# Decoder trunk: the key norm factors of eight heads as one set of rows

## The chip, the cores and the metric

One Trainium2 chip, one of its cores. The metric is the device time of one execution in microseconds (us), taken as the median of several runs. Engines: TensorE (PE, with its weight loads as PEld), VectorE (DVE), ScalarE (ACT), GpSimd (POOL) and SyncE (SP), whose queue issues nearly all DMAs.

## The reference

Two decoder layers over T = 528 tokens (16 learned meta tokens and 512 of the sequence), width 1024. Each layer normalises its input, projects it once, and runs two causal mixers side by side: a pooling mixer and a latent attention with 8 heads. The part that matters here is the norm of the keys in the attention:

```python
q = (c_q @ w_q_b).reshape(B, L, N_HEADS, QK_HEAD_DIM)          # QK_HEAD_DIM = 64 + 32
kv = (c_kv @ w_kv_b).reshape(B, L, N_HEADS, QK_NOPE_DIM + V_HEAD_DIM)
k_nope, v = kv[..., :QK_NOPE_DIM], kv[..., QK_NOPE_DIM:]
k_pe = jnp.broadcast_to(k_rope_raw[:, :, None, :], (B, L, N_HEADS, QK_ROPE_DIM))
k = jnp.concatenate([k_nope, k_pe], axis=-1)
q = rmsnorm(q, g_qn)
k = rmsnorm(k, g_kn)          # one factor for each token and head
...
x = x + W_out( sigmoid(g_pool) * y_pool + sigmoid(g_mla) * y_mla )
```

So each of 8 heads has 528 factors, 1/sqrt(mean(k*k) + eps), by which its keys are multiplied.

## The kernel before

All products run in float32 split into a high and a low part: each weight tile is a `whi`, `wlo` pair (L185, L186), each activation a pair too, and `mm3` (L190 to L192) issues three matrix products for each tile and column range. Activations lie with channels on the 128 partitions and tokens along the free side. Layer 0 works on 528 tokens in two halves of 264 columns, layer 1 (the last) on most projections with the 512 sequence tokens at once.

The order is written by hand in `Layer.go`: a generator (`stream`) yields the large products one after another with a cost each, and the attention's steps are put between them. `fill_now(ns)` runs so many nanoseconds of products before the next step, `after(ns, ...)` defers a step. The tile framework then schedules all engines' instructions with a timeline of its own, so small changes can move neighbours. Buffers rotate: `tmp` has 3, the PSUM tiles `mm` have 4, `S` (scores) 3, `raw` (weights as loaded) 3, `bc` 3.

The stage of the change is `qk_stats` (L653), once in each layer, after the queries' last product. The sums of squares of queries and keys are transposed to tokens on partitions (L672, L673), `newton` (L293 to L300) takes the inverse roots into `ny`, 128 partitions x 5 token groups x 16 (columns 0 to 7 the keys' heads, 8 to 15 the queries'). Group 4 holds the 16 meta tokens. The queries' factors stay like this (`nqs`). The keys' factors must become rows of 528 tokens, one for each head. For that, `qk_stats` makes two widened copies of the keys' factors, each a zero-filled tile (L692) with 5 groups of 97 columns, in which the four heads' factors stand in columns 0, 32, 64 and 96 (L694). `fill_now(9500)` follows. Then, for each of the two copies, `rows` transposes the five groups on TensorE (L404, L406 three times, L407) into two PSUM tiles, copies them with two activations (L409, L410) to a `tmp` tile of 97 partitions, and a DMA writes its rows 0, 32, 64 and 96 to DRAM (`kdr`, L700).

`spread_k(h)` (L707) reads one head's row from `kdr` back, broadcast to 128 partitions (`bc`, 264 KB): heads 0 and 1 at the end of the stage, each later one when `prep` of the head two before it runs. `prep(h)` (L711) multiplies the key parts by `bc` on VectorE (L718) and GpSimd (L719), splits the product into `kh` and `kl` (L280, L281, in `split`), splits the queries, and `head(h)` runs the scores (`S`, L190 to L192 through `mm3`) and the softmax. The products that run beside this stage are those of the pooling's up projection (`pu`, inputs `u`, `th`, `tl`, evacuated at L557) and of a gate (`zm`, inputs `hh`, `hl`, evacuated at L500 to L503).

SyncE's queue takes, in this stage, weight loads (`raw`, L114), the two writes of `kdr` and the broadcasts, in program order.

Of the kernel before, what the change touches and what calls it, by code (L numbers as in the profile page):

```python
# [9 lines left out]
F32 = mybir.dt.float32  # L10
# [8 lines left out]
P = 128  # L19
DEPTH = 2  # L20
# [3 lines left out]
T = SEQ + NM  # L24
# [3 lines left out]
H = 8  # L28
# [43 lines left out]
def trunk(ctx, tc, xT, pos, win, wkr, wqb, wkb, wvb, wgr, wpu, wmu, wout, gains, const, yT):  # L72
    nc = tc.nc
    pe, act, dve, gp, sp = nc.tensor, nc.scalar, nc.vector, nc.gpsimd, nc.sync
# [6 lines left out]
    dp = ctx.enter_context(tc.tile_pool(name="dp", bufs=1, space=bass.MemoryType.DRAM))  # L81
# [4 lines left out]
    def nm(s):  # L86
        uid[0] += 1
        return f"{s}_{uid[0]}"

    def slot(tag, dt=F32, bufs=1, w=W):  # L90
        return sl.tile([P, w], dt, tag=tag, name=nm(tag), bufs=bufs)

    def tmp(w=W):
        return tp.tile([P, w], F32, tag="tmp", name=nm("tmp"), bufs=3)
# [4 lines left out]
    def mmt():  # L99
        return pp.tile([P, 512], F32, tag="mm", name=nm("mm"), bufs=4)  # L100
# [173 lines left out]
    def fill_now(ns):  # L274
        end = clk[0] + ns
        while clk[0] < end and step():
            pass
# [15 lines left out]
    def newton(y, a, t):  # L293
        dve.tensor_single_scalar(y.bitcast(I32), a.bitcast(I32), 1, op=ALU.logical_shift_right)
        dve.tensor_scalar(y.bitcast(I32), y.bitcast(I32), -1.0, float(0x5F3759DF), op0=ALU.mult, op1=ALU.add)
        dve.tensor_scalar(a, a, -0.5, None, op0=ALU.mult)
        for _ in range(3):
            dve.tensor_mul(t, y, y)
            dve.tensor_mul(t, t, a)
            dve.scalar_tensor_tensor(out=y, in0=t, scalar=1.5, in1=y, op0=ALU.add, op1=ALU.mult)  # L300
# [13 lines left out]
        dve.tensor_scalar(tcos, tcos, -2.0, 1.0, op0=ALU.mult, op1=ALU.add)  # L314

    scr = dp.tile([P, 8, SEQ], F32, name="scr")
    kdr = [[dp.tile([4, T], F32, name=f"kdr{l}{s}") for s in range(2)] for l in range(DEPTH)]

    hbuf = [(slot(f"hh{k}", F32R), slot(f"hl{k}", F32R)) for k in range(8)]

    class Layer:
# [331 lines left out]
        def qk_stats(self):  # L653
            fill_now(LAG + 100)
            while self.sq:
                self.stat_go()
            st = self.st
            sts = tmp()
            assert self.nsq == [12, 12] and not self.sq
            if self.last:  # L660
                dve.memset(sts[0:16, 0:NM], 1.0)
                spans = [(8, 0, 0, NM), (16, 0, NM, HALF), (16, 1, HALF, T)]
            else:
                spans = [(16, 0, 0, HALF), (16, 1, HALF, T)]
            for r, s, a, b in spans:
                g, o_ = 32 * s, HALF * s
                act.activation(sts[0:r, a:b], st[s][g:g + r, a - o_:b - o_], AF.Copy)
                dve.tensor_add(sts[0:r, a:b], st[s][g + 64:g + 64 + r, a - o_:b - o_], sts[0:r, a:b])
            fill_now(2600)
            stp = mmt()  # L670
            for j in range(4):
                pe.transpose(stp[:, 16 * j:16 * j + 16], sts[0:16, NM + P * j:NM + P * (j + 1)], ident[0:16, 0:16])  # L672
            pe.transpose(stp[0:16, 64:80], sts[0:16, 0:NM], ident[0:16, 0:16])  # L673
            na = sm.tile([P, 5, 16], F32, tag="na", name=nm("na"))
            ny = sm.tile([P, 5, 16], F32, tag="ny", name=nm("ny"))
            nt = sm.tile([P, 5, 16], F32, tag="nt", name=nm("nt"))
            dve.memset(na[:, 4, :], 1.0)
            dve.scalar_tensor_tensor(out=na[:, 0:4, :], in0=stp[:, 0:64].rearrange("p (a b) -> p a b", a=4),
                                     scalar=1.0 / QK,
                                     in1=cst[:, C_ADD:C_ADD + 16].unsqueeze(1).to_broadcast([P, 4, 16]),  # L680
                                     op0=ALU.mult, op1=ALU.add)
            dve.scalar_tensor_tensor(out=na[0:16, 4, :], in0=stp[0:16, 64:80], scalar=1.0 / QK,
                                     in1=cst[0:16, C_ADD:C_ADD + 16], op0=ALU.mult, op1=ALU.add)
            dve.scalar_tensor_tensor(out=na[:, :, 8:16], in0=self.eps.unsqueeze(2).to_broadcast([P, 5, 8]), scalar=EPS,
                                     in1=na[:, :, 8:16], op0=ALU.mult, op1=ALU.add)
            newton(ny, na, nt)
            self.nqs = sm.tile([P, 5, 8], F32, tag="nqs", name=nm("nqs"))
            dve.tensor_scalar(self.nqs, ny[:, :, 8:16], -1.0 / math.sqrt(QK), None, op0=ALU.mult)
            ws = []
            for s in range(2):  # L690
                w = tmp()
                gp.memset(w, 0.0)  # L692
                v = w[:, 0:485].rearrange("p (j c) -> p j c", c=97)
                dve.tensor_copy(v[:, :, 0:97:32], ny[:, :, 4 * s:4 * s + 4])  # L694
                ws.append(v)
            fill_now(9500)
            for s, v in enumerate(ws):
                t = tmp()
                self.rows(v, 97, t[0:97, 0:T])
                sp.dma_start(kdr[self.l][s], t[0:97:32, 0:T])  # L700
            self.bcs = {}
            for h in range(2):
                self.spread_k(h)
            if not self.last:
                self.smeta = sm.tile([NM, 8, NM], F32, tag="smeta", name=nm("smeta"))

        def spread_k(self, h):  # L707
            self.bcs[h] = bc = slot("bc", bufs=3)
            sp.dma_start(bc, kdr[self.l][h // 4][h % 4:h % 4 + 1, :].partition_broadcast(P))

        def prep(self, h):  # L711
            p, odd = h // 2, h % 2
# [415 lines left out]
```

## Time and profile before

| | |
|---|---|
| median of 3 runs | 801.98 us (801.45 to 802.34) |
| the profiled execution | 802.28 us, span 800.5 us |
| granted TensorE clock | 1.000 |
| TensorE busy | 792.9 us, 99% of the span |
| VectorE, ScalarE, GpSimd busy | 527.4, 416.9, 196.4 us |
| HBM | 97 GB/s over the span |

The span runs from the first to the last instruction. A row of the chain of waits gives start, duration and what held the path (engine, tile, line of the kernel); a row of an engine's timeline gives start, busy time, engine, line, operation, the tile written and those read, and in brackets the idle time before it with what ended it. Matrix products overlap in the pipeline, so their busy times are longer than their distance from each other. In a row of one line's instructions the three numbers are the shortest, middle and longest duration in ns.

### The profile page before, as it was taken

Reading aid. Unit: us, or ns where it says so; the run is one execution under the profiler, and the core shown is the slowest. Engines: PE = TensorE matmul, PEld = TensorE weight load, DVE = VectorE, ACT = ScalarE, POOL = GpSimd, SP = SyncE. Lnnn points to the kernel's source line nnn. Section 1 sums busy time; section 2 is a strip of 40 time slices with the busy share of each in tenths; the row PEclk is TensorE's granted clock in tenths of the full one; section 3 lists DMA queues with packets and bytes.
Section 4 is the critical chain, followed back from the end, with each engine's and each line's share of the span. In section 5 each row is a group of like instructions: output and inputs, shape, how many; then the busy total and the mean of one; then the engine's idle time right before and its main releaser. Section 6 shows DMA issues by size and latency. Waiting matters only on the chain.

```text
span 800.5 us, 14638 instructions
## 1 busy us (share of the span) xinstructions
PE 792.9 (99%) x5339; PEld 714.0 (89%) x5339; DVE 527.4 (66%) x1140; ACT 416.9 (52%) x947; POOL 196.4 (25%) x266
## 2 busy tenths in 40 slices
PE   9999999999999999999999999999999999999998
PEld 8889999999999999999997997877788888887887
DVE  5568767437679887585354686665467889665942
ACT  7455645545556665543254456446455666654421
POOL 1024404103333322142000163022024333410600
PEclk9999999999999999999999999999999999999999
DMA  6223233424222222234642222334253322222372
GB/s 240 74 69 93 71 100 90 110 83 143 83 87 87 80 67 67 81 91 142 181 143 73 73 87 86 92 86 119 82 154 97 100 77 79 76 69 78 92 232 97
DMA packets 48872, 80.71 MB, mean 101 GB/s; under 512 B 5904, under 2 KB 14480, under 8 KB 48800
## 3 DMA queue, kind: packets, MB, share of 16 engines
q1 hardware_dynamic: 48656, 79.52, 33.5%
q8 instruction: 42, 0.69, 0.4%
q14 instruction: 30, 0.25, 0.1%
q10 hardware_dynamic: 144, 0.26, 0.1%
HBM read 73.40 MB, written 4.23 MB: 97 GB/s over the span
## 4 chain that ended last, share of the span: by engine, by line
PE 96%; DMA 2%; DVE 1%; ACT 1%; issue 0%; POOL 0%; POOLq 0%
PE mm L190 28%; PE mm L192 28%; PE mm L191 27%; PE mm L813 2%; PE S L191 2%; PE S L192 1%; PE S L190 1%; PE o L819 1%; PE o L818 1%; PE mm L363 1%; PE S L472 1%; DMA xb<-xT 1%; DMA bc<-kdr 1%; PE mm L430 0%; DMA rinv<-win 0%; PE mm L406 0%
## 5 line engine op out<-in xcount | busy, mean ns | idle before, releaser
L190 PE MATMUL mm<-hh,whi 128*128 128x264 f32 (+2 forms) x1096 | 346.0, 318 | 0.4 <-ACT racc L827 0.2
L191 PE MATMUL mm<-hl,whi 128*128 128x264 f32 (+2 forms) x1096 | 343.5, 314 | 0.0
L192 PE MATMUL mm<-hh,wlo 128*128 128x264 f32 (+2 forms) x1096 | 342.0, 315 | 0.0
L186 DVE TENSOR_TENSOR wlo<-raw,whi 128x512 fp32r<-128x512 f32 (+2 forms) x251 | 185.5, 743 | 118.1 <-ACT whi L185 110.8
L185 ACT ACTIVATE whi<-raw 128x512 fp32r<-128x512 f32 (+2 forms) x251 | 150.3, 602 | 186.2 <-PE mm L191 131.1
L190 PEld LDWEIGHTS mm<-hh,whi 128*128 128x128 f32 x1096 | 205.6, 188 | 13.8 <-ACT racc L827 0.5
L191 PEld LDWEIGHTS mm<-hl,whi 128*128 128x128 f32 x1096 | 206.2, 188 | 12.2 <-issue 0.4
L192 PEld LDWEIGHTS mm<-hh,wlo 128*128 128x128 f32 x1096 | 205.0, 188 | 12.7 <-issue 0.4
L719 POOL TENSOR_TENSOR tmp<-kp,bc 64x528 f32<-64x528 f32 x16 | 24.5, 1532 | 113.2 <-DMA bc<-kdr 77.9
L550 POOL TENSOR_TENSOR racc<-racc,tmp 128x264 f32<-128x264 f32 (+1 forms) x15 | 14.1, 942 | 143.1 <-ACT tmp L549 143.0
L791 POOL TENSOR_TENSOR pm<-pa,rs 128x16 f32<-128x16 f32 x32 | 11.6, 361 | 145.6 <-DVE rs L786 145.6
L901 POOL TENSOR_TENSOR tmp<-tmp,xb 128x264 f32<-128x264 f32 (+1 forms) x24 | 26.9, 1143 | 58.6 <-DVE tmp L899 33.0
L747 DVE CUSTOM_DVE_ANT_0 S<-S,maskw,nqs 128x272 f32<-128x272 f32 (+4 forms) x80 | 38.4, 498 | 1.6 <-PE S L192 1.2
L754 ACT ACTIVATE cq<-S,bia 128x400 f32<-128x400 f32 (+2 forms) x48 | 24.6, 516 | 21.5 <-DVE bia L781 11.9
L190 PE MATMUL mm<-u,whi 128*128 128x264 f32 (+1 forms) x108 | 35.3, 327 | 0.0
L192 PE MATMUL mm<-cq,wlo 128*128 128x264 f32 (+1 forms) x108 | 34.8, 323 | 0.0
L192 PE MATMUL mm<-u,wlo 128*128 128x264 f32 (+1 forms) x108 | 34.8, 322 | 0.0
L191 PE MATMUL mm<-cq,whi 128*128 128x264 f32 (+1 forms) x108 | 34.8, 322 | 0.0
L190 PE MATMUL mm<-cq,whi 128*128 128x264 f32 (+1 forms) x108 | 34.7, 322 | 0.0
L281 DVE TENSOR_TENSOR tl<-mm,th 128x512 fp32r<-128x512 f32 (+1 forms) x64 | 29.3, 482 | 6.8 <-ACT th L280 5.8
L793 POOL TENSOR_TENSOR cq<-cq,rs 128x384 f32<-128x384 f32 (+1 forms) x32 | 32.7, 1021 | 0.0
L280 ACT ACTIVATE th<-mm 128x512 fp32r<-128x512 f32 (+1 forms) x64 | 25.4, 433 | 10.7 <-PE mm L813 10.4
(262 smaller groups left out, 1383.6 us busy)
## 6 DMA issues: line engine op xcount, KB each, us to landing
raw<-win SPq DMA_DIRECT2D x143, 256.0 KB, 2.6
raw<-wout SPq DMA_DIRECT2D x32, 256.0 KB, 3.0
bc<-kdr SPq DMA_DIRECT2D x16, 264.0 KB, 3.7
raw<-wpu SPq DMA_DIRECT2D x16, 256.0 KB, 2.6
raw<-wmu SPq DMA_DIRECT2D x16, 256.0 KB, 2.7
raw<-wqb SPq DMA_DIRECT2D x12, 256.0 KB, 2.8
tmp<-xT SPq DMA_DIRECT2D x16, 132.0 KB, 3.0
tmp<-scr SPq DMA_DIRECT2D x7, 256.0 KB, 4.3
```

The costliest lines, as they stand in the source:

```text
L185: act.activation(hi[:, :n], raw[:, :n], AF.Copy)
L186: dve.tensor_sub(lo[:, :n], raw[:, :n], hi[:, :n].bitcast(F32))
L190: pe.matmul(out, wh, xh, start=start, stop=False)
L191: pe.matmul(out, wh, xl, start=False, stop=False)
L192: pe.matmul(out, wl, xh, start=False, stop=stop)
L280: act.activation(hi[:, a:b], src, AF.Copy)
L281: dve.tensor_sub(lo[:, a:b], src, hi[:, a:b].bitcast(F32))
L719: gp.tensor_mul(kf[r0:r0 + 64, :], self.kp[r0:r0 + 64, :], bc[r0:r0 + 64, :])
L747: dve.tensor_tensor_reduce(out=sv, in0=sv, in1=mask, scale=nqs[:, i, h:h + 1], scalar=3e38, op0=ALU.add, op1=ALU.min, accum_out=bia[:, c:c ...
L754: act.activation(pv, sv, AF.Exp, scale=-1.0, bias=bia[:, i:i + 1], accum_out=rs[:, c:c + 1])
L793: gp.tensor_mul(pt[i][:, NM:], pt[i][:, NM:], rs[:, i:i + 1].to_broadcast([P, n - NM]))
L901: gp.tensor_add(t[:, :b - a], t[:, :b - a], self.am[m][:, a:b])
```

## The change

The two widened copies, their zero fills and the second pass of `rows` go. The keys' factors, columns 0 to 7 of each group in `ny`, are transposed directly: one set of five transposes with 8 columns each, two activations on 8 partitions, and one DMA that writes all eight rows to one `kdr` tile of 8 x 528 for each layer. `spread_k` reads its row from there. `rows` itself is the same; it also serves `norm_sums`, with 34 columns, as before.

```diff
-    kdr = [[dp.tile([4, T], F32, name=f"kdr{l}{s}") for s in range(2)] for l in range(DEPTH)]
+    kdr = [dp.tile([H, T], F32, name=f"kdr{l}") for l in range(DEPTH)]
...
-            ws = []
-            for s in range(2):
-                w = tmp()
-                gp.memset(w, 0.0)
-                v = w[:, 0:485].rearrange("p (j c) -> p j c", c=97)
-                dve.tensor_copy(v[:, :, 0:97:32], ny[:, :, 4 * s:4 * s + 4])
-                ws.append(v)
             fill_now(9500)
-            for s, v in enumerate(ws):
-                t = tmp()
-                self.rows(v, 97, t[0:97, 0:T])
-                sp.dma_start(kdr[self.l][s], t[0:97:32, 0:T])
+            t = tmp()
+            self.rows(ny[:, :, 0:8], 8, t[0:8, 0:T])
+            sp.dma_start(kdr[self.l], t[0:8, 0:T])
             self.bcs = {}
             for h in range(2):
                 self.spread_k(h)
...
         def spread_k(self, h):
             self.bcs[h] = bc = slot("bc", bufs=3)
-            sp.dma_start(bc, kdr[self.l][h // 4][h % 4:h % 4 + 1, :].partition_broadcast(P))
+            sp.dma_start(bc, kdr[self.l][h:h + 1, :].partition_broadcast(P))
```

## The prediction

> **What bounds the kernel now.** The page comes first: its busy times, then the chain that ended last. The profiled execution took 802.28 us, 1.78 us of it outside its span of 800.5 us.
>
> ```profile
> span 800.5 us, 14638 instructions
> PE 792.9 (99%) x5339; PEld 714.0 (89%) x5339; DVE 527.4 (66%) x1140; ACT 416.9 (52%) x947; POOL 196.4 (25%) x266
> PE 96%; DMA 2%; DVE 1%; ACT 1%; issue 0%; POOL 0%; POOLq 0%
> ```
>
> TensorE works 99% of the span and carries 96% of the chain. So a time on TensorE counts one for one, and a time on VectorE, ScalarE or GpSimd counts only where TensorE waits for it. The two places to read are the factor stages, once per layer (near 175 us and 577 us): the statistics are transposed into rows, written to DRAM (`kdr`), read back as broadcasts (`bc`), multiplied into the keys and split (`kh`, `kl`), and then the first scores run. The chain of waits in the first layer, in order of time (start, duration, what):
>
> ```profile
> 174.47 0.18 PE mm L404
> 174.65 0.50 PE mm L406 x3
> ...
> 175.79 0.26 ACT whi L185
> 176.05 0.28 issue
> 176.33 0.26 ACT tmp L410
> 176.59 0.03 ACT xb L557
> 176.61 1.72 DMA kdr<-tmp
> 178.33 0.02 issue
> 178.35 4.70 DMA bc<-kdr
> ...
> 183.21 1.76 POOL tmp L719
> 184.97 0.02 issue
> 184.99 0.65 ACT kh L280
> 185.64 0.04 issue
> 185.69 0.58 PE S L190 x2
> 186.26 0.12 PE mm L192
> ```
>
> This chain leaves TensorE for ScalarE at 175.79 and comes back to it at 185.69: the first scores of layer 0 wait for the factor's round trip through DRAM. TensorE's own timeline gives the size of that wait:
>
> ```profile
> 185.69 0.58 PE L190 MATMUL S<-kh,qhl 128*128 128x272 f32 x2 [0.49 <-ACT kh L280]
> ```
>
> It idles 0.49 us there; the products that the order puts ahead of the scores hide the rest of the trip. In layer 1 the chain stays on TensorE through the same stage:
>
> ```profile
> 576.00 0.18 PE mm L404
> 576.18 0.50 PE mm L406 x3
> 576.68 0.11 PE mm L407
> ...
> 577.72 0.18 PE mm L404
> 577.91 0.50 PE mm L406 x3
> 578.41 0.11 PE mm L407
> ...
> 587.76 0.31 PE S L190 x2
> ```
>
> Both sets of five transposes stand on the path, and the scores at 587.76 wait for nothing. ScalarE's row for their operand shows the slack:
>
> ```profile
> 584.80 0.65 ACT L280 ACTIVATE kh<-tmp 128x528 fp32r<-128x528 f32 x1 [2.58 <-POOL tmp L719]
> ```
>
> `kh` is done at 585.45, 2.31 us ahead. So one edit meets two limits: layer 1 is bound by TensorE's work, layer 0 by a DMA chain.
>
> **The work that goes.** Off the path first: four zero fills on GpSimd and four copies on VectorE leave.
>
> ```profile
> L694 DVE COPY tmp<-ny x4: 171/172/174, 169.4 to 571.0; 128x20 f32<-128x20 f32 x4
> ```
>
> The copies are 4 x 0.17 us, the first of layer 0 begun at 169.4 us; the transposes that read them run at 174.47, because `fill_now(9500)` puts products ahead of them, not because the copies end late. The fills come ahead of the copies (same buffers) on an engine that is 25% busy. Cost and gain of both are zero; what hides them is those 5 us of products. Two of four activations per layer (L409, L410) also go, from a ScalarE that is 52% busy; the second pair never stood in the chain. Of `tmp` buffers a layer takes three fewer, and with three in rotation every later user gets the buffer it had.
>
> On TensorE ten transposes go, five per layer, and the ten left load 8 columns of weights instead of 97. No row shows 8 columns. The nearest is the same helper on 34 columns (the chain, earlier in layer 0):
>
> ```profile
> 40.41 0.12 PE mm L404
> 40.53 0.43 PE mm L406 x3
> 40.96 0.11 PE mm L407
> ```
>
> and the weight loads of L404 and of L472 (min, median, max in ns):
>
> ```profile
> L404 PEld LDWEIGHTS mm<-cst,tmp x6: 91/156/156, 40.3 to 577.7; 16*97 16x97 f32 x4, 16*34 16x34 f32 x2
> L472 PEld LDWEIGHTS S<-sq,cst x88: 92/96/98, 72.3 to 562.4; 128*16 128x16 f32 x88
> ```
>
> A set of 97 columns costs 0.18 + 0.50 + 0.11 = 0.79 us of the path, one of 34 columns 0.12 + 0.43 + 0.11 = 0.66. From 34 columns to 16 the load stays at 91 to 92 ns at best, so I take 0.66 for 8 columns; bounds are 0.79 (no cheaper) and 0.60 (the straight line through 97 and 34 carried on to 8). The Trainium skill (TensorE: Matmul & The Clock Gate, "Step-by-step: what each phase is for") says that the weight load's time scales with the column count. By that rule an 8-column load would be an estimated 91 x 8 / 34 = 21 ns, and five of them would take up to 0.35 us more off each set, an estimated gain of 0.7 us beyond my sum if the load alone set the pace. The 34- and 16-column rows speak against it: the load has a floor, and I leave that out.
>
> **Layer 1.** Two sets of 0.79 become one of 0.66: 1.58 - 0.66 = 0.92 us (bounds 0.79 and 0.98). The built program's order puts the first four transposes two products earlier and leaves the fifth, which the write waits for, where the first set's was. The gain counts in full if the scores still find `kh` ready. SyncE's queue there:
>
> ```profile
> 577.42 0.54 SPq L700 DMA_DIRECT2D kdr<-tmp  x1
> 579.14 0.33 SPq L709 DMA_DIRECT2D bc<-kdr  x1
> ```
>
> The second write stood between the first and the second broadcast; it goes, and three broadcasts follow each other at once, as they already do in layer 0. The first broadcast waits for the write (579.14 - 577.42 = 1.72 us), as before. TensorE comes 0.92 us earlier, so the slack falls from 2.31 to 1.39 us. The broadcasts' landing is between these ends:
>
> ```profile
> DMA to landing us min/median/max: 3.0/3.7/5.3
> ```
>
> In layer 1 the first one took about 3.1 us (issued 579.14, its reader on VectorE starts at 582.26):
>
> ```profile
> 582.26 0.70 DVE L718 TENSOR_TENSOR tmp<-kn,bc 64x528 f32<-64x528 f32 x1 [3.38 <-DMA bc<-kdr]
> ```
>
> At layer 0's 4.70 it would be 1.6 us later, just 0.2 us over the slack. I take no wait; the bound is that one is 0.2 us, or 0.8 us with a landing of 5.3.
>
> **Layer 0.** Here the saved TensorE time meets a wait. The order of the built program shows one move: the first scores now stand four 264-column products later (they follow the third weight pass of `hh3`, where they stood after the second product of `hh2`). A product is 0.12 us (row 186.26), four are 0.48. Without waits TensorE would come to the scores at 185.69 - 0.49 (the idle) - 0.92 (the work) + 0.48 (the four) = 184.76. The chain does not come that early. Up to the weight-split activation it gains what the first four transposes save: 0.18 + 0.50 - 0.12 - 0.43 = 0.13 us, since L185 is released by the product behind them and L410 by the fifth transpose. From there nothing is shortened: the write, the broadcast, GpSimd's multiply, the split. The second write left SyncE's queue, but the broadcast was waiting for the first one's landing (1.72 here, 1.72 in layer 1 where nothing stood between). So the scores start at 185.69 - 0.13 = 185.56 and TensorE idles 0.8 us instead of 0.49. What counts is the place in the work: at 185.56 four more products are done than before at 185.69. The gain is 0.13 + 0.48 = 0.61 us, not the 1.41 us (0.92 of work, 0.49 of idle) that the transposes promise. `kl` and the next scores keep their five products of distance.
>
> What is unknown is the write of eight rows on one tile. Rows for both sides: the four-row write, 1.72 us in both layers, and the 66 KB moves of 32 rows:
>
> ```profile
> qhl<-q SPq DMA_DIRECT2D x16, 66.0 KB, 2.0
> ```
>
> That bounds it by 1.72 and 2.0; eight rows of 16.5 KB lie by the first, and I take 1.72. The loss is at most 0.28 us, in layer 0 alone. The Trainium skill (DMA: Bandwidth & Descriptors, "Why a DMA increments its semaphore by 16 and not by 1") has it that a copy is spread over the largest number of engines up to 16 that divides its row counts: eight rows would use eight engines where four used four, one row each, and last no longer. No view here shows the engines of one write.
>
> **Sum.** 0.92 + 0.61 = 1.53 us. 802.28 - 1.53 = 800.75 for the profiled execution's kind; that run was 0.30 us over the median of 801.98, so against the median 801.98 - 1.53 = 800.45, said as 800.4. The difference that a measurement can tell is 0.2%, or 1.6 us: my forecast lies just inside that.
>
> **Rivals.**
> *The broadcast comes sooner (0.22).* In layer 0 the first broadcast took 4.70 us, in layer 1 3.1, the median is 3.7. Ahead of it stand a 256 KB weight load and, between the two, the second write, which goes. If that write was what held it by a microsecond, TensorE's wait vanishes and layer 0 gains 0.92 + 0.49 = 1.41. The whole is 2.33 us, 799.65. Against it: the weight load stays ahead, 8 KB are little.
> *The factors come later and take the gain back (0.08).* A write of 2.0 us and a broadcast of 5.3 in both layers: layer 0 loses 0.28 + 0.60, layer 1 is 0.28 + 2.2 later and beyond its slack by 1.1. The gain is 1.53 - 0.88 - 1.1, -0.4: 802.4, no difference to be told.
> *Slower (0.11).* The one larger write lands late, and both layers wait for it. Each microsecond costs layer 0 in full, layer 1 from 1.39 us on. The gain is gone at 1.5 us of lateness (a write of 3.2 us), and from 2.3 us on (4.0 us) it is slower by more than 1.6. At the 5.3 us of the slowest broadcast, 3.58 us late, it is 1.53 - 3.58 - 2.19: 4.2 us slower, 806.2. Against it: the 66 KB moves take 2.0.
> *The change does less on TensorE:* 0.79 for a set makes 0.79 in layer 1 and 0.48 in layer 0, 1.27 us and 800.7. This lies in the forecast's case.
>
> **The numbers.** The forecast has 0.59, split by the 1.6 us bound: its gain runs from 1.27 (sets no cheaper) to 1.75 (sets of 0.60, which make 0.98 and 0.67, and a broadcast 0.1 us sooner), 0.26 of it beyond 1.6 and 0.33 within. Faster: 0.26 + 0.22 = 0.48. Same: 0.33 + 0.08 = 0.41. Slower: 0.11. The range runs from 799.4 (the first rival with the cheapest sets, 0.06 in each layer, and 0.1 for the spread of the runs) to 801.7 (the forecast with the write and the broadcast late in layer 0, 0.88, and the runs' spread above their median, 802.34 - 801.98 = 0.36); left out are the slower rival and a part of the late one.
>
> **What would show it.** In the profile after: in each layer one L404, three L406 and one L407 with 8 rows out, a set of 0.66 us in the chain; four fewer GpSimd fills; in layer 0 the wait of the first scores for `kh` up to about 0.8 us, at 1 us earlier in TensorE's work; the broadcast about 1.7 us after the write; in layer 1 no wait at the first scores. The forecast is wrong if the wait in layer 0 is gone (sooner broadcast) or over 1.5 us (late write), or if a wait for `kh` appears in layer 1.

## The result and the profile after

| | before | after | ratio, 95% interval |
|---|---|---|---|
| first comparison, median | 801.71 us (8 runs) | 799.54 us (8 runs) | 0.9971 [0.9962, 0.9980] |
| second, another group of runs | 801.56 (20) | 800.20 (10) | 0.9974 [0.9965, 0.9984] |
| third | 801.33 (13) | 799.55 (9) | 0.9977 [0.9967, 0.9987] |

The change makes the kernel faster by 0.23 to 0.29% by the ratios, 1.4 to 2.2 us by the medians (the ratios are not formed from these medians and come to 1.8 to 2.3 us). The mean of all 27 runs after lies 1.9 us below that of all 41 before. Forecast were 1.53 us (0.19%), just inside what was taken for the smallest difference that can be told. The profiled execution took 799.36 us, its span is 797.6 us. Its page (span, busy times, chain by engine):

```profile
span 797.6 us, 14595 instructions
PE 790.3 (99%) x5329; PEld 711.8 (89%) x5329; DVE 528.1 (66%) x1136; ACT 416.0 (52%) x943; POOL 194.4 (24%) x262
PE 96%; DMA 2%; ACT 1%; DVE 1%; issue 0%; POOL 0%; ACTq 0%; POOLq 0%
```

Nothing else became the bound: TensorE still has 96% of the chain, with ten products fewer. The chain of waits through layer 0's stage (start, duration, what):

```profile
174.17 0.11 PE mm L404
174.28 0.42 PE mm L406 x3
...
175.35 0.63 ACT whi L185
175.98 0.16 ACT tmp L410
...
176.16 1.47 DMA kdr<-tmp
...
177.65 4.43 DMA bc<-kdr
...
182.21 1.79 POOL tmp L711
...
184.03 0.65 ACT kh L280
...
184.72 0.58 PE S L190 x2
```

It is the same chain as before, and TensorE waits at its end as before (its own timeline):

```profile
184.72 0.58 PE L190 MATMUL S<-kh,qhl 128*128 128x272 f32 x2 [0.41 <-ACT kh L280]
```

In layer 1 one set is left on the path, in two parts, and the first scores wait for nothing:

```profile
573.65 0.11 PE mm L404
573.76 0.42 PE mm L406 x3
...
574.65 0.11 PE mm L407
```

```profile
583.21 0.65 ACT L280 ACTIVATE kh<-tmp 128x528 fp32r<-128x528 f32 x1 [3.83 <-POOL tmp L711]
584.77 0.47 PE L190 MATMUL S<-kh,qhl 128*128 128x272 f32 x2
```

`kh` is ready at 583.86, the scores start at 584.77.

**Where the time sits.** Two marks in each layer enclose the stage: the first transpose of the statistics (L672) and the first group of transposed probabilities (L813 before, L805 after). Rows of the chain, before and then after:

```profile
162.63 0.16 PE mm L672
203.18 0.77 PE mm L813 x7
565.26 0.35 PE mm L672 x4
605.35 0.55 PE mm L813 x5
```

```profile
162.33 0.16 PE mm L672
201.74 0.76 PE mm L805 x7
563.38 0.35 PE mm L672 x4
602.51 0.55 PE mm L805 x5
```

The stage went from 40.55 to 39.41 us in layer 0 (1.14 us) and from 40.09 to 39.13 us in layer 1 (0.96 us). The first gain is almost twice what was forecast (0.61), the second is near the forecast 0.92. The other 0.8 us between the two spans are the start (0.30 us up to the first mark), the stretch between the stages (0.44) and what comes behind them (0.06).

**What the wait costs.** The number in brackets is the idle time from the end of one record to the start of the next. Here a matrix product's record lasts 0.28 us while the next one starts 0.12 us after it, so the bracket leaves out a part of the pause. TensorE's rows around layer 0's first scores, in the first trace of the kernel before and in a second one (e8 below):

```profile
184.92 0.28 PE L191 MATMUL mm<-hl,whi 128*128 128x264 f32 x1
185.69 0.58 PE L190 MATMUL S<-kh,qhl 128*128 128x272 f32 x2 [0.49 <-ACT kh L280]
186.10 0.28 PE L192 MATMUL mm<-hh,wlo 128*128 128x264 f32 x1
```

```profile
185.24 0.29 PE L191 MATMUL mm<-hl,whi 128*128 128x264 f32 x1
185.37 0.47 PE L190 MATMUL S<-kh,qhl 128*128 128x272 f32 x2
185.68 0.29 PE L192 MATMUL mm<-hh,wlo 128*128 128x264 f32 x1
```

In e8 nothing waits: `kh` is done 0.20 us ahead, the scores start 0.13 us after the product before them, and the next product 0.31 us after the scores. In the first trace these distances are 0.77 and 0.41 us, so the wait cost 0.64 + 0.10 = 0.74 us of TensorE's time, not the 0.49 of the bracket. In each of the other twelve traces the scores start 0.05 or 0.06 us after `kh` is done, so there TensorE waits for it, even where no bracket is shown. The marks and this cost were read in every run below:

| kernel | stage 0 | idle in brackets | cost of the wait | stage 0 without the cost | stage 1 |
|---|---|---|---|---|---|
| before, three traces | 40.55, 39.82, 39.96 | 0.49, 0, 0 | 0.74, 0, 0.16 | 39.81, 39.82, 39.80 | 40.09, 40.09, 40.09 |
| after, three traces | 39.41, 39.89, 39.43 | 0.41, 0.90, 0.43 | 0.66, 1.15, 0.69 | 38.75, 38.74, 38.74 | 39.13, 39.14, 39.13 |
| e1, adjacent rows | 40.93 | 0.87 | 1.12 | 39.81 | 40.12 |
| e2, two writes | 39.06 | 0 | 0.31 | 38.75 | 39.14 |
| e3, two narrow sets | 40.79 | 0.90 | 1.16 | 39.63 | 39.76 |
| e4, one wide set | 40.09 | 0.93 | 1.19 | 38.90 | 39.28 |
| e5, rows two apart | 39.41 | 0.37 | 0.63 | 38.78 | 39.16 |
| e6 and e11, fill_now(10200) | 38.33, 38.57 | 0, 0.25 | 0.26, 0.50 | 38.07, 38.07 | 39.14, 39.14 |

(us.) Without the cost of the wait each kernel's stage 0 repeats to 0.02 us; with the brackets alone taken off, the kernel before would have 40.06, 39.82 and 39.96. The stage of e6 and e11 holds 313 products, that of the kernel after 319, so these two are not to be compared: six products have moved behind its second mark. Two other stretches of TensorE's work repeat to 0.02 us in all thirteen traces: start of the norm sums to the first mark 137.98 to 138.00, second mark of layer 1 to the last head's end 117.18 or 117.19. The stretch between the two stages does not: 361.56 to 362.08.

### The profile page after: what moved, and what is told of

It reads as the page before. It is cut to its first block, busy times and chain, and to the rows that moved or that the text cites. A ratio compares the mean times of both kernels' runs of the same rounds, so it can differ in the third digit from the quotient of the medians.

```text
span 797.6 us, 14595 instructions
## 1 busy us (share of the span) xinstructions
PE 790.3 (99%) x5329; PEld 711.8 (89%) x5329; DVE 528.1 (66%) x1136; ACT 416.0 (52%) x943; POOL 194.4 (24%) x262
## 4 chain that ended last, share of the span: by engine, by line
PE 96%; DMA 2%; ACT 1%; DVE 1%; issue 0%; POOL 0%; ACTq 0%; POOLq 0%
PE mm L190 28%; PE mm L192 27%; PE mm L191 27%; PE mm L805 2%; PE S L191 2%; PE S L192 2%; PE S L190 1%; PE o L811 1%; PE o L810 1%; PE mm L363 1%; PE S L472 1%; DMA xb<-xT 1%; DMA bc<-kdr 1%; PE mm L430 0%; DMA rinv<-win 0%; DMA raw<-wmu 0%
```

## The experiments

Theories. A: the write of the kernel before was slow to issue because its source rows lie apart; that it does not do so any more made layer 0's chain shorter than forecast. Rivals: B, eight rows on one DMA go faster than four; C, the second write in the queue held the first broadcast; D, the gain comes from narrow weights, not from the count of sets. Then E and F, on the broadcast's landing.

**e1, adjacent rows.** The kernel before, with

```diff
-                dve.tensor_copy(v[:, :, 0:97:32], ny[:, :, 4 * s:4 * s + 4])
+                dve.tensor_copy(v[:, :, 0:4], ny[:, :, 4 * s:4 * s + 4])
...
-                sp.dma_start(kdr[self.l][s], t[0:97:32, 0:T])
+                sp.dma_start(kdr[self.l][s], t[0:4, 0:T])
```

> The kernel before, with the four heads' factors in columns 0 to 3 of each widened copy instead of 0, 32, 64 and 96, and the two writes from rows 0 to 3. Still 97 columns, two sets, two writes. The order puts layer 0's first scores two 264-column products earlier than before. Theory A (the write of the kernel before was slow to issue because its source rows lie 32 partitions apart): the write's issue takes 0.3 us instead of 0.54 to 0.59, and in layer 0 the broadcast is issued 1.5 us after the write instead of 1.74; the two products fewer leave the wait for the key operand at about 0.5 us, so the time is that of the kernel before within 0.2 us. Theory B (eight rows go faster than four): issue 0.54, 1.74 us, the wait 0.73 us, 0.25 us slower than before.

Measured: 802.34 us, ratio 1.0012 [1.0003, 1.0021], slower by 0.7 us by the medians. The write's issue on SyncE's queue, in ns, for the kernel before, e1, the kernel after, e4 and e5 (rows 32 apart, adjacent, adjacent, 12 apart, 2 apart):

```profile
L700 SPq DMA_DIRECT2D kdr<-tmp x4: 537/542/595, 176.6 to 579.5; - x4
```

```profile
L700 SPq DMA_DIRECT2D kdr<-tmp x4: 267/320/330, 176.4 to 579.5; - x4
```

```profile
L692 SPq DMA_DIRECT2D kdr<-tmp x2: 292/321/350, 176.2 to 575.1; - x2
```

```profile
L696 SPq DMA_DIRECT2D kdr<-tmp x2: 677/696/714, 176.3 to 576.3; - x2
```

```profile
L696 SPq DMA_DIRECT2D kdr<-tmp x2: 670/688/707, 175.9 to 575.3; - x2
```

In e1 the broadcast was issued 1.42 us after the write (176.36 to 177.78) instead of 1.74. So A holds for the write: adjacent rows alone bring it, with four rows and two writes, and B falls. The idle time of 0.87 us was missed (0.5 expected), and the likely cause is in two rows, GpSimd's multiply in e1 and in the kernel after:

```profile
182.38 2.46 POOL L719 TENSOR_TENSOR tmp<-kp,bc 64x528 f32<-64x528 f32 x1 [40.10 <-PE mm L191]
```

```profile
182.21 1.78 POOL L711 TENSOR_TENSOR tmp<-kp,bc 64x528 f32<-64x528 f32 x1 [40.93 <-DMA bc<-kdr]
```

VectorE's timeline in e1 in that time:

```profile
182.34 0.70 DVE L718 TENSOR_TENSOR tmp<-kn,bc 64x528 f32<-64x528 f32 x1 [5.45 <-DMA bc<-kdr]
182.97 0.68 DVE L186 TENSOR_TENSOR wlo<-raw,whi 128x512 fp32r<-128x512 f32 x1
```

A weight's low part follows VectorE's multiply at once, and GpSimd's multiply takes 0.68 us longer, just the length of that operation. In the kernel after no second VectorE operation stands there. The Trainium skill (SBUF — State Buffer, "Who interferes with whom") has it that a VectorE instruction with two SBUF inputs contends with a GpSimd instruction that reads SBUF, and that this contention is an exclusive lock. These rows agree: one operation of 0.68 us for 0.68 us.

**e2, two writes.** The kernel after, with

```diff
-            sp.dma_start(kdr[self.l], t[0:8, 0:T])
+            for s in range(2):
+                sp.dma_start(kdr[self.l][s], t[4 * s:4 * s + 4, 0:T])
```

and two `kdr` tiles read as before.

> The kernel after, but the eight rows are written by two DMAs of four adjacent rows, to two DRAM tiles as before. One narrow set of transposes. The order puts layer 0's first scores eight products (0.97 us) later than in the kernel after. Theory A: issue 0.3 us for each write, broadcast 1.5 us after the first; the eight products cover the rest of the DMA chain, no wait for the key operand in layer 0, 0.4 us faster than the kernel after, 2.2 to 2.6 us faster than before. Theory C (the second write in the queue is what held the broadcast of the kernel before): the first broadcast lands 0.3 us or more later than in the kernel after (4.7 us after its issue, not 4.43); the time is the same as in theory A since 0.5 us of cover are left.

Measured: 799.15 us, ratio 0.9975 [0.9966, 0.9984], 2.5 us faster by the medians. No idle time in brackets, but the scores start 0.34 us after the product before them, so a wait of 0.31 us is left, where none was expected. Stage 0 is 39.06, and without the wait 38.75, the same as the kernel after. The broadcast came 1.42 us after the first write (176.94 to 178.36) and landed 4.51 us later in the chain, between 4.43 and 4.92 of the kernel after. One trace in such a spread could not show the 0.3 us that C expects. But the kernel before, with its second write, has the two shortest landings of all traces with a load between write and broadcast (e8 and e9), so C falls. Layer 1's stage is the same as in the kernel after (39.14): one DMA instead of two is no part of the gain on TensorE.

**e3, two narrow sets.** The kernel after, with

```diff
-            t = tmp()
-            self.rows(ny[:, :, 0:8], 8, t[0:8, 0:T])
-            sp.dma_start(kdr[self.l], t[0:8, 0:T])
+            for s in range(2):
+                t = tmp()
+                self.rows(ny[:, :, 4 * s:4 * s + 4], 4, t[0:4, 0:T])
+                sp.dma_start(kdr[self.l][s], t[0:4, 0:T])
```

> The kernel after, but two narrow sets of five transposes with 4 columns each, two pairs of activations and two writes of four adjacent rows: no widened copies, but nothing merged. The order puts layer 0's first scores six products (0.73 us) earlier than in the kernel after. Theory A: layer 1 gives back one set, 0.64 us, and keeps 0.3 of its gain of 0.95; in layer 0 the chain is as short as in the kernel after and the wait grows to 0.5 us, which with six products fewer keeps 0.4 of its 1.14 us. Sum 0.7 us faster than before. Theory D (the gain is the narrow weights, not the count of sets): 2 us faster than before, layer 1 keeps 0.7 us or more.

Measured: 801.22 us, ratio 1.0000 [0.9991, 1.0009], 0.4 us faster by the medians, where A expected 0.7. Layer 1 keeps 0.33 of 0.96 us, as A said (0.3), not 0.7 (D). The 0.4 us of layer 0 did not come: the idle time was 0.90 us, with GpSimd's multiply beside two VectorE operations again (2.35 us in its row of the chain), and its products alone took 0.26 us more than 38.74 + 0.63, which was not taken apart.

**e4, one wide set.** The kernel after, with one widened copy of 85 columns:

```diff
+            w = tmp()
+            gp.memset(w, 0.0)
+            v = w[:, 0:425].rearrange("p (j c) -> p j c", c=85)
+            dve.tensor_copy(v[:, :, 0:85:12], ny[:, :, 0:8])
             fill_now(9500)
             t = tmp()
-            self.rows(ny[:, :, 0:8], 8, t[0:8, 0:T])
-            sp.dma_start(kdr[self.l], t[0:8, 0:T])
+            self.rows(v, 85, t[0:85, 0:T])
+            sp.dma_start(kdr[self.l], t[0:85:12, 0:T])
```

> The kernel after, but the eight heads' factors stand in columns 0, 12, ... 84 of one widened copy of 85 columns, so that there is one set of wide transposes and one write whose eight source rows lie 12 partitions apart. The order puts layer 0's first scores one product later than in the kernel after. Theory A: the write's issue takes 0.5 us or more and the broadcast comes 1.74 us or more after it; a set costs 0.76 us; layer 0 gains 0.9, layer 1 0.83, 1.7 us faster than before. Theory B (eight rows go faster than four): issue 0.3 us, 1.5 us, layer 0 gains 1.1, 1.95 us faster. Theory D: 0.3 us faster than before.

Measured: 800.01 us, ratio 0.9983 [0.9974, 0.9992], 1.64 us faster by the medians. Layer 1 gains 0.81 (0.83 expected); D is out. The issue takes 0.68 to 0.71 us, the broadcast came 1.81 us after the write (176.28 to 178.09): with eight rows apart the write is slower than with four. Layer 0 gained 0.46 instead of 0.9, with an idle time of 0.93 us and a broadcast of 4.78.

From e3 and e4 the parts of layer 1's 0.96 us: a second narrow set 0.63 us (39.76 - 39.13), the width 0.33 us in two sets (40.09 - 39.76) or 0.15 in one of 85 columns.

**e5, rows two apart.** The same with 15 columns, `v[:, :, 0:15:2]`, and `t[0:15:2, 0:T]` as the source.

> The kernel after, but the eight heads' factors stand in columns 0, 2, ... 14 of one widened copy of 15 columns: narrow weights, one set, one write, its source rows two partitions apart. The order puts layer 0's first scores one product later than in the kernel after, layer 1's one later too. Theory A1 (any step between the source rows makes the write slow to issue, and what follows it slow): issue 0.7 us, broadcast issued 1.8 us after the write and landing 4.7 to 4.8 us later as with a step of 12; the wait for the key operand about 0.9 us, layer 0 gains 0.5 us over before, layer 1 0.95, 1.4 us faster than before. Theory A2 (only rows far apart are slow): issue 0.3, 1.5 and 4.45 us as in the kernel after, wait 0.3 us, layer 0 gains 1.2, 2.2 us faster than before.

Measured: 800.18 us, ratio 0.9984 [0.9974, 0.9993], 1.4 us faster by the medians. The issue is as slow as with a step of 12 (row above), and the broadcast came 1.87 us after the write (175.93 to 177.80): a step of 2 costs as much as one of 12, so it is not the distance that counts (A1). But in this trace the broadcast landed in 4.15 us, not 4.7 to 4.8, and stage 0 was as short as in the first trace of the kernel after. So the broadcast's landing does not follow from the write, and is a question by itself.

**e6, another place of the transposes.** The kernel after with `fill_now(10200)` for 9500.

> The kernel after with fill_now(10200) in place of 9500. In layer 0 the transposes move six products later, eighty products instead of 78 stand between them and the first scores, and on SyncE's queue no weight load stands between the write and the broadcasts; layer 1's order is as in the kernel after. Theory E (the first broadcast of layer 0 takes 4.43 us because a 256 KB load is ahead of it): it lands in 3.1 to 3.5 us, the first scores wait for nothing, layer 0 gains 0.4 us more, 2.5 us faster than before. Rival (a load ahead of the write only moves the delay from the broadcast to the write): broadcast 2.3 us after the write, 3.3 us to land, a wait of about 0.3 us, 2.2 us faster than before.

Measured: 799.08 us, ratio 0.9963 [0.9950, 0.9976], the fastest so far. SyncE's queue and the first scores:

```profile
177.56 0.37 SPq L692 DMA_DIRECT2D kdr<-tmp  x1
179.89 1.29 SPq L701 DMA_DIRECT2D bc<-kdr  x3
```

```profile
183.06 0.70 DVE L710 TENSOR_TENSOR tmp<-kn,bc 64x528 f32<-64x528 f32 x1 [2.34 <-DMA bc<-kdr]
```

```profile
185.58 0.65 ACT L280 ACTIVATE kh<-tmp 128x528 fp32r<-128x528 f32 x1 [2.39 <-POOL tmp L711]
```

```profile
185.99 0.28 PE L191 MATMUL mm<-hl,whi 128*128 128x264 f32 x1
186.28 0.57 PE L190 MATMUL S<-kh,qhl 128*128 128x272 f32 x2
```

Without a load between write and broadcast, the broadcast's first reader starts 3.17 us after its issue; but the write, now with a load issued 0.38 us ahead of it (177.18), takes 2.33 us. Both E and its rival fit: the load would delay whichever DMA stands behind it. This is argued from these rows, not shown. In layer 1, where a load is issued 1.63 us ahead of the write both here and in the kernel after, the write took 1.47 us here and 2.27 there, so the order in the queue does not settle its time. Write and broadcast together take 5.50 us, 5.94 in the kernel after's first trace. The idle time in brackets is gone, but the wait is not, against E: `kh` is done at 186.23, the scores start 0.05 us later and 0.29 us after the product before them. The wait still costs 0.26 us, near the rival's 0.3.

**e7, the kernel after again**, unchanged.

> The kernel after, unchanged, for a second trace. The stage of layer 0 and that of layer 1 take what they took (the gains of 1.14 and 0.95 us over before); the start of the run and the stretch behind the first layer's stage, which were 0.3 and 0.46 us shorter than before, show by how much they vary: if the change shortened them they come out the same, if it is spread they differ by a few tenths.

Measured: 800.20 us, ratio 0.9974 [0.9965, 0.9984]. Layer 1's stage came out the same (39.14). Layer 0's did not: 39.89, with an idle time of 0.90 us. The chain names it:

```profile
176.46 1.48 DMA kdr<-tmp
177.93 0.02 issue
177.95 4.92 DMA bc<-kdr
```

The write took what it took in the first trace (1.47), the broadcast half a microsecond more. The start (24.65 us against 24.35) and the stretch between the stages (361.89 against 361.64) were both longer than in the first trace, so what they had gained there is at least in part spread.

**e8 and e9, the kernel before again**, unchanged.

> The kernel before, unchanged, for a second trace of it. Theory F (the first broadcast of layer 0 lands at varying times from run to run, 4.2 to 4.9 us after its issue, in either kernel; the change has no part in it; what the change shortens is the write, by a quarter of a microsecond): the write leads the broadcast by 1.72 to 1.74 us in both layers as in the first trace, the landing differs from 4.70 by some tenths and layer 0's stage, from the statistics' first transpose to the first transposed probabilities, by as much from 40.55 us; layer 1's stage is 40.09 us again. Rival (the change also shortens the broadcast): 4.70 and 40.55 again.

> The same, for a third trace: theory F again a landing of its own between 4.2 and 4.9 us; the rival 4.70 and 40.55.

Measured: 801.52 and 802.12 us. SyncE's queue in e8 and the broadcast's first reader (the first scores are shown further up):

```profile
176.94 0.60 SPq L700 DMA_DIRECT2D kdr<-tmp  x1
177.64 0.34 SPq L114 DMA_DIRECT2D raw<-win  x1
...
178.68 1.32 SPq L709 DMA_DIRECT2D bc<-kdr  x3
```

```profile
182.60 0.70 DVE L718 TENSOR_TENSOR tmp<-kn,bc 64x528 f32<-64x528 f32 x1 [1.16 <-DMA bc<-kdr]
```

The write leads the broadcast by 1.74 us in layer 0 in all three traces of before. The broadcast's first reader starts 4.72, 3.92 and 4.14 us after its issue, and the wait costs 0.74, 0 and 0.16 us. F holds in that the landing varies in both kernels (after: 4.45, 4.94, 4.46), but more widely than its 4.2 to 4.9 us. From the write's issue to that reader it is 6.46, 5.66 and 5.88 us before, 5.94, 6.43 and 5.96 us after: on the mean 6.0 and 6.1, the same. So on these means the write's quarter of a microsecond does not reach the keys, though three traces each that scatter by half a microsecond and more could hide it. Theory A explains the write, not the stage. That the broadcast, issued sooner, only waits longer behind the same weight load is the likely reading; it is argued from e6, not shown by itself.

**e10, the kernel after a third time, and e11, fill_now(10200) again**, on one chip.

> The kernel after, unchanged, for a third trace, and timed on the same chip as the next. Theory F: write to broadcast 1.47 to 1.49 us in layer 0 as in both traces so far, landing between 4.2 and 4.9, layer 0's stage between 39.1 and 39.9 us, layer 1's 39.14. About 2 us faster than before. Rival: landing near 4.43.

> The kernel after with fill_now(10200), again, beside the kernel after on one chip. Theory F with the wait gone: layer 0's stage is 38.3 us again whatever the broadcast's landing, since nothing waits for it, and the time is 0.7 to 1.3 us less than that of the kernel after. Rival (the first trace was a lucky landing): a wait for the key operand of some tenths, the time of the kernel after.

Measured: e10 799.55 us (799.08 to 800.65), ratio 0.9977 [0.9967, 0.9987]; e11 798.69 us (798.50 to 799.65), ratio 0.9962 [0.9950, 0.9975]. e10: write to broadcast 1.50 us, stage 0 39.43. e11 is 0.86 us below e10 by the medians, as e6 was 1.1 us below e7, also on one chip. The landing was not without effect, against F's word: TensorE sat idle 0.25 us, and the wait cost 0.50. So `fill_now(10200)` is the version that is faster than both kernels in the two places where they ran side by side; against the kernel before the intervals of the two overlap. Of its gain over the kernel after, the shorter wait is 0.45 us on the means (0.38 against 0.83 us); the rest was not taken apart.

## Why the prediction was right or wrong

**Layer 1: right.** 0.92 forecast, 0.95 to 0.96 measured in three traces each. A set of 8 columns takes 0.11 + 0.42 + 0.11 = 0.64 us of the path against 0.66 taken from 34 columns. No wait came; the slack by TensorE's own row fell to 0.91 us in the first trace (by the same row, 587.60, it was 2.15 before, so 1.23 was to be left), since the write there took 2.27 us (issued 575.09, broadcast 577.36; 1.88 and 1.90 in e7 and e10), a delay for which the prediction had no term. Its cause is open: with the same order in layer 1, e6 and e11 show 1.47 and 1.48 us. The first trace's rows:

```profile
575.09 0.29 SPq L692 DMA_DIRECT2D kdr<-tmp  x1
577.36 1.27 SPq L701 DMA_DIRECT2D bc<-kdr  x3
```

**The weights' floor: right.** The prediction let the load's time stay near 91 ns instead of falling with the columns. By the Trainium skill (TensorE: Matmul & The Clock Gate, "Step-by-step: what each phase is for") 8 columns were an estimated 21 ns. The loads of L404 and L406 in the kernel after, 34 columns and 8:

```profile
L404 PEld LDWEIGHTS mm<-cst,tmp x2: 91/92/92, 40.0 to 444.8; 16*34 16x34 f32 x2
L404 PEld LDWEIGHTS mm<-cst,ny x2: 77/78/78, 174.1 to 573.6; 16*8 16x8 f32 x2
L406 PEld LDWEIGHTS mm<-cst,ny x6: 83/87/87, 174.2 to 573.8; 128*8 128x8 f32 x6
```

The time falls with the columns, but only by 14 ns from 34 to 8, so the trace does not bear out the 21 ns.

**Layer 0: the mechanism right, three sizes off.** The prediction held that the chain through DRAM, not TensorE's work, sets the time here, and that four products more ahead of the scores are part of the gain. So it is: in all three traces of the kernel after, the scores start as soon as `kh` is done. The step that failed is this one: "From there nothing is shortened: the write, the broadcast, GpSimd's multiply, the split." In the first pair of traces the stage gained 1.14 us where the term was 0.61. The path up to the write gave 0.15 (0.13 forecast) and the four products 0.48, but the write took 1.47 us and not 1.72, and the broadcast 4.43 and not 4.70.

The write is the first size, and it lasts: 1.47 to 1.50 us from write to broadcast in all three traces, since the issue of adjacent rows takes 0.3 us instead of 0.55 (e1). The broadcast is the second. Its 4.70 us, read from one execution, were taken as the kernel's own; they were a slow draw, and so were 0.27 us of that gain. The third is the wait: the 0.49 us were the bracket, where the wait cost 0.74 in that trace and 0.30 on the mean of three.

On these means TensorE's work in stage 0 falls from 39.81 to 38.74, by 1.07 us, and the wait's cost grows from 0.30 to 0.83. So layer 0 gains 0.53 us, where 0.61 was forecast; by the scatter of the waits this is known to some 0.3 us. That the two agree is in part luck: the write's quarter of a microsecond was left out, and the broadcasts' first readers came 0.36 us later after the change (4.62 against 4.26 on the mean), which nothing in the forecast held.

**The sum and the call.** The sum's size is near what was measured, and the call made from it is wrong. It rests on the sentence "The difference that a measurement can tell is 0.2%, or 1.6 us: my forecast lies just inside that." The intervals came to 0.1% on either side, 0.7 to 0.8 us, and the kernel after is faster in all three comparisons. The forecast lay 0.07 us inside its own bound and was taken for no difference, although its own chances had "faster" (0.48) ahead of "same" (0.41). The medians say 2.2, 1.4 and 1.8 us; by the first interval the gain is 1.6 to 3.0 us, so the forecast lies just under it, and inside the other two (1.3 to 2.8, 1.0 to 2.6).

By the means of all runs the gain is some 0.4 us more than the forecast. The traces show where it may lie, not why. The spans of the three traces each are 1.97 us apart on the mean: 0.53 in stage 0, 0.96 in stage 1, 0.31 at the start, 0.09 between the stages and 0.07 behind them. The two stages make 1.5 us, as forecast. The start up to the norm sums is 24.35, 24.65 and 25.24 us after against 24.64, 24.96 and 25.57 before; over all traces it goes from 24.08 to 25.57, and nothing in the change reaches it, so three traces can't tell its 0.31 us from chance.

**The rivals.** That the broadcast comes sooner: it did in the first trace (4.43) and not in the second (4.92), so there is no lasting effect, and the kernel before landed sooner still with its second write in the queue (e8, e9). That the factors come later and take the gain back: in layer 1 the write took up to 0.55 us longer, within the slack. Slower by a late write: in layer 0 eight adjacent rows took 1.47 to 1.50 us, four adjacent 1.42, four rows apart 1.74. That a set is no cheaper: it costs 0.64 us, not 0.79. The range, 799.4 to 801.7, held all three medians.

## What to carry to other kernels

Work taken from the bounding engine ahead of a DMA round trip is paid out in full only if the trip stays covered: count the saved work, then ask which wait it uncovers, and move the trip's start or the cover with it, as `fill_now(10200)` does here. A wait that is read in one profile is one draw: two more profiles of the unchanged kernel (0.74, 0 and 0.16 us) would have sized this term better than any reasoning on the change. Where records overlap, read a wait from start to start, against a trace or a layer that has none. Put the rows of a small write on adjacent partitions: its issue is shorter, though these traces show no gain of the stage from it.

## What the runs showed of the hardware

A DMA whose source rows are not on adjacent partitions was slower to issue from SyncE's queue: 0.27 to 0.37 us for four or eight adjacent rows, 0.54 to 0.60 for four rows 32 apart, 0.67 to 0.71 for eight rows 2 or 12 apart. The broadcast followed the write of the kernel after by 1.47 to 1.50 us in layer 0, where the last weight load was issued 2.9 us ahead of the write, by 2.25 and 2.33 us with a load 0.4 us ahead (layer 0 of e6 and e11), and by 1.47 to 2.27 us with one 1.6 us ahead (layer 1, five traces); what sets it was not shown. With a load between write and broadcast the broadcast's first reader started 3.9 to 4.9 us after its issue, without one 3.1 to 3.5 us.

A wait of TensorE cost more than the idle time between its records: products of 264 columns start 0.12 us apart while each record lasts 0.28 us, and in the twelve traces with a wait the product behind the first scores also starts 0.41 or 0.42 us after them instead of 0.31.
